# Second feed-forward of a two-layer trunk: the up projection by seven block products, the down projection as one long sum in PSUM

## The chip, the cores and the metric

One core of a Trainium2 chip runs one program. The metric is the device time of one execution in microseconds.

## The reference, cut to what matters

Two layers over 1024 tokens of width 1024, float32. Each layer is a mixer and then a convolutional feed-forward; only the feed-forward of layer 1, the last stage but for a final norm, is touched.

```python
def conv_ffn(h, w_in, conv_w, conv_b, w_out):     # h 1024 x 1024, w_in 1024 x 5632, w_out 2816 x 1024
    up = h @ w_in
    val, gate = jnp.split(up, 2, axis=-1)         # 2816 each
    gate = causal_depthwise_conv(gate, conv_w, width=3) + conv_b
    return (jax.nn.gelu(gate) * val) @ w_out
...
    h = modulated_rmsnorm(x, norm2_g[i], sh2, sc2)
    x = x + g2[:, None, :] * conv_ffn(h, ffn_w_in[i], ffn_conv_w[i], ffn_conv_b[i], ffn_w_out[i])
return rmsnorm(x, final_g).astype(x.dtype)
```

## The kernel before, in words

All activations lie transposed: 128 channels on the partitions, tokens along the free side, in two halves of 512 tokens (`hf`). The residual xT has eight tiles of 128 channels (`KD`). Each float32 factor of a product is split into a rounded high part and a low rest (`split`, L101: ScalarE copies the high part, L105, VectorE subtracts, L106), and one product is three matmuls, high by high, high by low and low by high (`mm3`, L109, its matmuls L115 to L117). So a tile of the up projection over one half is 8 x 3 matmuls of 128 x 512.

The feed-forward (`ffn`, L1382) goes over 11 pairs of tiles (22 tiles of 128, `NF`). For a pair and a half, `up` multiplies two gate and two value tiles, `gate` does the three taps and the GELU, `value` multiplies and splits the result. `down` multiplies the pair's two tiles with the weights of all eight output tiles and adds each sum to xT right away (L1451). Gate and value stay in SBUF. The normed input of half 0 is made during the output projection of half 1 (`out_proj1`, L1375), that of half 1 during the first four up products (`norm_parts`, L566, whose three parts are the sum of squares, the row factors by `rstd_cols` and Newton steps, and the spread over the partitions, L551, with the scaling). At the end `finish` (L1477) transposes each half back, norms it and stores it.

A planner fixes each engine's order before the run, by the order of the code; `high_priority(offset=...)` moves a block's instructions forward by that many. A buffer of a pool is taken again when all that used it is done; the memory of a closed pool is reused in the same way, tile by tile. Loads go through SyncE's queue (SP), stores and re-loads of x through GpSimd's (POOL); each queue issues in its order. In `out_proj` (L1358) the reads of xT (L1370) are put behind the weight loads on SP.

## Time and profile before

| | |
|---|---|
| median of 3 runs | 2573.07 us (2572.48 to 2581.45) |
| profiled execution | 2570.86 us |
| its span, first to last instruction | 2569.2 us |
| mean granted TensorE clock | 0.988 |
| up and down of the second feed-forward on TensorE | from about 1824 us to about 2553 us |

The span is in microseconds from the first instruction. PE is the TensorE matmuls, PEld its weight loads, DVE VectorE, ACT ScalarE, POOL GpSimd, SPq the issue queue of SyncE. A row's line is that of the code; where a helper records the operation, the names of its operands tell the place: `up` and `dn` are the sums of the two projections, `lin` those of the output projection, `h` the normed input, `wH` and `wL` the split weights.

### The profile page before, as it was taken

The page shows a single profiled execution, that of the slowest core. Times are in us where ns is not written, and L with a number is a line of the kernel's source. Part 1 is how long each engine was busy: PE and PEld are TensorE (multiplying, and loading weights), DVE is VectorE, ACT ScalarE, POOL GpSimd, SP SyncE. Part 2 cuts the span into 40 slices and gives each one's busy share as a digit, 9 for nine tenths or more (in the row PEclk, how much of TensorE's full clock was granted, in tenths as well). Part 3 has the DMA queues.
Part 4 walks back from the last instruction along what each step waited for, and adds up shares of the span by engine and source line. Part 5 has one row for each costly group of instructions (what it writes and reads, how often), then busy time and mean ns, then how long its engine had stood idle before and what let it go on. Part 6 is the DMA issues. An engine that isn't in the chain of part 4 may idle for free.

```text
span 2569.2 us, 32004 instructions
## 1 busy us (share of the span) xinstructions
PE 2500.7 (97%) x12127; PEld 2076.3 (81%) x12127; DVE 1580.3 (62%) x3085; ACT 913.9 (36%) x1521; POOL 134.5 (5%) x252
## 2 busy tenths in 40 slices
PE   6999999999999999999999999999999999999998
PEld 5788888887788888888888778787788888888886
DVE  6777776666845595567678554664744444444447
ACT  3655566673322232212224333332421222222222
POOL 1000000040000000000001121210000000000000
PEclk7999999999999999999999999899999999999999
DMA  8455544476412333332233442426211111111111
GB/s 300 132 143 144 149 136 134 140 247 204 143 50 81 102 109 107 110 94 81 81 101 124 152 152 85 154 97 227 75 57 42 49 49 50 45 46 44 47 50 66
DMA packets 260922, 282.43 MB, mean 110 GB/s; under 512 B 21345, under 2 KB 191958, under 8 KB 260256
## 3 DMA queue, kind: packets, MB, share of 16 engines
q1 hardware_dynamic: 240576, 211.64, 27.4%
q0 software_dynamic: 20192, 68.75, 7.7%
q8 instruction: 95, 1.56, 0.3%
q14 instruction: 59, 0.48, 0.1%
HBM read 213.04 MB, written 40.94 MB: 99 GB/s over the span
## 4 chain that ended last, share of the span: by engine, by line
PE 83%; DVE 5%; DMA 4%; issue 3%; ACT 3%; POOL 0%; SPq 0%; DVEq 0%; ACTq 0%; POOLq 0%
PE up L115 12%; PE up L117 12%; PE up L116 12%; PE dn L115 6%; PE dn L117 6%; PE dn L116 6%; PE lin L115 6%; PE lin L116 6%; PE lin L117 6%; PE ta L709 1%; PE S L686 1%; DMA mix<-mixd 1%; PE S L687 1%; DMA pn<-in_mod_w_dram 1%; PE ta L535 1%
## 5 line engine op out<-in xcount | busy, mean ns | idle before, releaser
L115 PE MATMUL up<-h,wH 128*128 128x512 f32 x1408 | 549.7, 390 | 3.0 <-DVE xT L1372 3.0
L116 PE MATMUL up<-h,wH 128*128 128x512 f32 x1408 | 548.1, 389 | 0.0
L117 PE MATMUL up<-h,wL 128*128 128x512 f32 x1408 | 547.9, 390 | 0.2 <-DVE wL L106 0.2
L1451 DVE SCALAR_TENSOR_TENSOR xT<-dn,mod,xT 128x512 f32<-128x512 f32 x352 | 261.4, 748 | 122.0 <-PE dn L117 120.7
L106 DVE TENSOR_TENSOR wL<-stage,wH 128x1024 fp32r<-128x1024 f32 x164 | 199.8, 1221 | 210.3 <-ACT wH L105 206.6
L115 PEld LDWEIGHTS up<-h,wH 128*128 128x128 f32 x1408 | 264.3, 188 | 58.8 <-issue 2.0
L117 PEld LDWEIGHTS up<-h,wL 128*128 128x128 f32 x1408 | 264.3, 188 | 56.1 <-DVE wL L106 1.0
L116 PEld LDWEIGHTS up<-h,wH 128*128 128x128 f32 x1408 | 264.5, 188 | 54.9
L105 ACT ACTIVATE wH<-stage 128x1024 fp32r<-128x1024 f32 x164 | 173.1, 1058 | 310.2 <-PE lin L116 108.2
L115 PE MATMUL dn<-gh,dH 128*128 128x512 f32 x704 | 275.4, 392 | 0.2 <-ACT dH L105 0.2
L117 PE MATMUL dn<-gh,dL 128*128 128x512 f32 x704 | 274.6, 391 | 0.1
L116 PE MATMUL dn<-gl,dH 128*128 128x512 f32 x704 | 274.6, 390 | 0.0
L115 PE MATMUL lin<-h,wH 128*128 128x512 f32 x576 | 235.0, 408 | 7.4 <-ACT h L403 6.6
L116 PE MATMUL lin<-h,wH 128*128 128x512 f32 x576 | 233.9, 406 | 0.0
L117 PE MATMUL lin<-h,wL 128*128 128x512 f32 x576 | 230.6, 401 | 0.0
L1397 ACT ACTIVATE ca<-up,colsB,taps 128x512 f32<-128x512 f32 x84 | 64.9, 772 | 392.1 <-PE up L117 391.9
L115 PEld LDWEIGHTS dn<-gh,dH 128*128 128x128 f32 x704 | 132.1, 188 | 28.6 <-ACT dH L105 0.9
L117 PEld LDWEIGHTS dn<-gh,dL 128*128 128x128 f32 x704 | 132.2, 188 | 27.7 <-DVE dL L106 0.5
L116 PEld LDWEIGHTS dn<-gl,dH 128*128 128x128 f32 x704 | 132.4, 188 | 27.2 <-DVE gl L1415 0.2
L1413 DVE TENSOR_TENSOR ca<-up,ca 128x512 f32<-128x512 f32 x84 | 57.8, 690 | 148.5 <-PE up L117 145.3
L1398 DVE SCALAR_TENSOR_TENSOR ca<-up,taps,ca 128x511 f32<-128x511 f32 x84 | 62.6, 746 | 134.8 <-ACT ca L1397 134.6
L115 PEld LDWEIGHTS lin<-h,wH 128*128 128x128 f32 x576 | 110.6, 192 | 28.8 <-ACT h L403 6.9
(452 smaller groups left out, 3929.8 us busy)
## 6 DMA issues: line engine op xcount, KB each, us to landing
stage<-in_ffn_w_in_dram SPq DMA_DIRECT2D x88, 512.0 KB, 3.8
pn<-in_mod_w_dram SPq DMA_DIRECT2D x160, 256.0 KB, 3.0
stage<-in_ffn_w_out_dram SPq DMA_DIRECT2D x44, 512.0 KB, 3.3
mix<-mixd POOLq DMA_DIRECT2D x60, 256.0 KB, 5.7
stage<-in_ev_w_in_dram SPq DMA_DIRECT2D x24, 512.0 KB, 4.0
mixd<-t2k POOLq DMA_DIRECT2D x44, 256.0 KB, 3.1
mw<-in_mod_w_dram SPq DMA_DIRECT2D x32, 256.0 KB, 5.2
Q<-pn SPq DMA_DIRECT2D x64, 128.0 KB, 2.3
```

The costliest lines, as they stand in the source:

```text
L105: nc.scalar.activation(wh[:, :n], st[:, :n], AF.Copy)
L106: nc.vector.tensor_tensor(wl[:, :n], st[:, :n], f(wh[:, :n]), ALU.subtract)
L115: nc.tensor.matmul(ps, wh, xh, start=s, stop=False)
L116: nc.tensor.matmul(ps, wh, xl, start=False, stop=False)
L117: nc.tensor.matmul(ps, wl, xh, start=False, stop=e)
L535: nc.tensor.matmul(p[:, t:t + 1], accs[t // 4][:, t % 4 * 128:t % 4 * 128 + 128], self.ones, start=True, stop=True)
L686: nc.tensor.matmul(dst, q, KH[:, kk], start=True, stop=False)
L687: nc.tensor.matmul(dst, q, KL[:, kk], start=False, stop=True)
L1397: nc.scalar.activation(a, p, AF.Identity, bias=self.cb[l][:, ft:ft + 1], scale=w2)
L1398: v.scalar_tensor_tensor(a[:, 1:512], p[:, 0:511], w1, a[:, 1:512], ALU.mult, ALU.add)
L1413: nc.vector.tensor_tensor(a, p, a, ALU.mult)
L1451: nc.vector.scalar_tensor_tensor(xT[:, n, hs], p, g2[:, n:n + 1], xT[:, n, hs], ALU.mult, ALU.add)
```

## The change

The up projection of layer 1 is computed by Winograd's form of Strassen's scheme on 2 x 2 blocks. The weights of a tile are four blocks: gate and value (g, v) by the lower and the upper half of the 1024 input channels. The input is four blocks: lower and upper channels by token half (B11, B12 / B21, B22). With T1 = B12 - B11, T2 = B22 - T1, T3 = B22 - B12, T4 = B21 - T2 and S = v_lo + v_hi, the seven products are p1 = g_lo B11, p2 = g_hi B21, p3 = (g_hi - S + g_lo) B22, p4 = v_hi T4, p5 = S T1, p6 = (S - g_lo) T2, p7 = (g_lo - v_lo) T3; the four results are p1 + p2, p1 + p6 + p5 + p3, p1 + p6 + p7 + p4 and p1 + p6 + p7 + p5. Each product is four blocks of 128 by three matmuls.

`up7_blocks` makes the T blocks in place of the normed xT, with a split of each; the first half's norm also writes its result into xT (`keep`), so x is stored to DRAM first (`store_x`) and loaded again for the down projection. The first four tiles (`PRE`) run p1 and p2 ahead. Gate times value goes to DRAM (`Gd`). `down22` runs after all of up: for each half and each group of four output tiles it sums all 22 tiles in four PSUM banks; weights (512 columns) and gate-value (512 columns) are loaded into one stage buffer and split together. There are six stage buffers and three pairs of split buffers. In the output projection before it, the second pair of weight buffers lies in X0 (`Slots`, views of one tile handed out in turn), and xT and the new blocks lie at other addresses than before. `conv` is the taps and GELU as in `gate`, from SBUF. The feed-forward of layer 0 is as it was.

```diff
+PRE = 4
...
         for d in range(KD):
-            t = self.tmp()
+            t = xT[:, d, hs] if keep else self.tmp()
             h, lo = self.hx(d, hf)
             nc.vector.scalar_tensor_tensor(t, xT[:, d, hs], gs[:, d:d + 1], r, ALU.mult, ALU.mult)
-            nc.scalar.activation(h, t, AF.Identity, bias=sh[:, d:d + 1])
-            nc.vector.scalar_tensor_tensor(lo, t, sh[:, d:d + 1], f(h), ALU.add, ALU.subtract)
+            if keep:
+                nc.scalar.activation(t, t, AF.Identity, bias=sh[:, d:d + 1])
+                nc.scalar.activation(h, t, AF.Copy)
+                nc.vector.tensor_tensor(lo, t, f(h), ALU.subtract)
+            else:
+                nc.scalar.activation(h, t, AF.Identity, bias=sh[:, d:d + 1])
+                nc.vector.scalar_tensor_tensor(lo, t, sh[:, d:d + 1], f(h), ALU.add, ALU.subtract)
 
...
-    def out_proj1(self, w, l, xT, x, ps, fetch=False):
-
-        parts = self.norm_parts(xT, 0, l, 1, ps, "lin")
+    def out_proj1(self, w, l, xT, x, ps, fetch=False, keep=False):
+
+        if keep:
+            self.store_x(xT, 0)
+        parts = self.norm_parts(xT, 0, l, 1, ps, "lin", keep)
         next(parts)
         self.out_proj(w, l, xT, 1, x, ps, between=parts, fetch=fetch)
...
+    def up7_blocks(self, l, xT, ps, tag, xb):
+        nc, v = self.nc, self.nc.vector
+        gs, sh = self.gs[l][:, 8:16], self.mod[l][:, 24:32]
+        h0, h1 = slice(0, 512), slice(512, 1024)
+        acc = self.sumsq(xT, h1)
+        yield
+        y = self.rstd_cols([acc], D, ps, tag)
+        yield
+        r = self.spread_cols(y, ps, tag)
+        self.h[1] = X1 = self.new_h(1, "h")
+        X0, X2 = self.xblocks
+        B11, B12, B21, B22 = (xT[:, k:k + 4, h] for k in (0, 4) for h in (h0, h1))
+        T1, T3, T4, T2 = X1[:, :, 0:4], X1[:, :, 4:8], X2[:, :, 0:4], X2[:, :, 4:8]
+        def scale(k):
+            for d in range(k, k + 4):
+                t = xT[:, d, h1]
+                v.scalar_tensor_tensor(t, t, gs[:, d:d + 1], r, ALU.mult, ALU.mult)
+                nc.scalar.activation(t, t, AF.Identity, bias=sh[:, d:d + 1])
+        def low(x, dst):
+            nc.scalar.activation(dst[:, 0], x, AF.Copy)
+            v.tensor_tensor(dst[:, 1], x, f(dst[:, 0]), ALU.subtract)
+        scale(0)
+        v.tensor_tensor(B11, B12, B11, ALU.subtract)
+        scale(4)
+        low(B11, T1)
+        low(B22, X0)
+        v.tensor_tensor(B12, B22, B12, ALU.subtract)
+        v.tensor_tensor(B22, B22, B11, ALU.subtract)
+        low(B22, T2)
+        v.tensor_tensor(B21, B21, B22, ALU.subtract)
+        low(B12, T3)
+        low(B21, T4)
+        yield
+    def up7(self, l, blocks, free, wxs, Gd):
+        nc, v, i = self.nc, self.nc.vector, self.i
+        wi = i["ffn_w_in"][l]
+        def load(pool, n0):
+            st = pool.tile([128, 1024], F32, tag="stage", name="stage", bufs=2)
+            nc.sync.dma_start(st.rearrange("p (t n) -> p t n", n=128),
+                              wi[:, n0:n0 + 128].rearrange("(t p) n -> p t n", p=128))
+            return st
+        with self.pool(f"u7ps{l}", bufs=1, space=PSUM) as ps:
+            bank = lambda k: ps.tile([128, 512], F32, tag=f"c{k}", name=f"c{k}", bufs=(0, 2, 3, 3)[k])
+            prep = blocks(ps, bank)
+            X = {}
+            def operands():
+                h0, X1 = self.h
+                X0, X2 = self.xblocks
+                X.update(B22=at(X0, range(4)), T1=at(X1, range(4)), T3=at(X1, range(4, 8)),
+                         T4=at(X2, range(4)), T2=at(X2, range(4, 8)))
+            at = lambda t, k: [(t[:, 0, n], t[:, 1, n]) for n in k]
+            X.update(B11=at(self.h[0], range(4)), B21=at(self.h[0], range(4, 8)))
+            def product(p, W, o, x, start=True, stop=True):
+                self.mm3(p, [(W[0][:, o + j * 128:o + j * 128 + 128], W[1][:, o + j * 128:o + j * 128 + 128]) + X[x][j]
+                             for j in range(4)], start, stop)
+            def head(ft, q, again=False):
+                with self.tc.high_priority(offset=AHEAD):
+                    early = 2 <= ft < PRE
+                    q["g"] = load(wxs if early and not again else self.wp, (NF + ft) * 128)
+                    if not again:
+                        q["A"] = self.split(q["g"], 1024, *((self.wp, "w", 2) if ft < PRE and ft % 2 else (wxs, "w", 1)))
+            def p1(ft, q):
+                p = bank(1)
+                product(p, q["A"], 0, "B11")
+                q["s1"] = self.tmp(tag="pn")
+                nc.scalar.copy(q["s1"], p)
+            def p2(ft, q):
+                q["c1"] = bank(1)
+                product(q["c1"], q["A"], 512, "B21")
+            def sums(ft, q):
+                with self.tc.high_priority(offset=AHEAD):
+                    g, a = q["g"], load(wxs, ft * 128)
+                    q["s3"] = s3 = self.tmp(tag="ma")
+                    lo, hi = slice(0, 512), slice(512, 1024)
+                    v.tensor_tensor(s3, g[:, lo], a[:, lo], ALU.subtract)
+                    v.tensor_tensor(a[:, lo], a[:, lo], a[:, hi], ALU.add)
+                    q["V"] = self.split(a, 1024, late)
+                    v.tensor_tensor(g[:, lo], a[:, lo], g[:, lo], ALU.subtract)
+                    v.tensor_tensor(g[:, hi], g[:, hi], g[:, lo], ALU.subtract)
+                    q["G"] = self.split(g, 1024, self.wp)
+            def conv(ft, hf, p, q):
...
+            def out(ft, hf, a, val):
+                v.tensor_tensor(a, val, a, ALU.mult)
+                nc.gpsimd.dma_start(Gd[ft][:, hf * 512:hf * 512 + 512], a)
+            def gate0(ft, q):
+                c = self.tmp(tag="ma")
+                v.tensor_tensor(c, q["c1"], q["s1"], ALU.add)
+                q["a0"] = conv(ft, 0, c, q)
+            def p5(ft, q):
+                p = bank(3)
+                product(p, q["V"], 0, "T1")
+                q["s5"] = self.tmp()
+                nc.scalar.copy(q["s5"], p)
+            def p3(ft, q):
+                q["c3"] = bank(3)
+                product(q["c3"], q["G"], 512, "B22")
+            def third(ft, q):
+                with self.tc.high_priority(offset=AHEAD):
+                    q["S3"] = [late.tile([128, 512], F32R, tag=t, name=t, bufs=1) for t in ("s3h", "s3l")]
+                    nc.scalar.activation(q["S3"][0], q["s3"], AF.Copy)
+                    v.tensor_tensor(q["S3"][1], q["s3"], f(q["S3"][0]), ALU.subtract)
+            def p6(ft, q):
+                p = bank(2)
+                product(p, q["G"], 0, "T2")
+                q["u2"] = late.tile([128, 512], F32, tag="u2", name="u2", bufs=1)
+                v.tensor_tensor(q["u2"], p, q["s1"], ALU.add)
+            def p7(ft, q):
+                p = bank(2)
+                product(p, q["S3"], 0, "T3")
+                q["u3"] = late.tile([128, 512], F32, tag="u3", name="u3", bufs=1)
+                v.tensor_tensor(q["u3"], p, q["u2"], ALU.add)
+            def p4(ft, q):
+                p = bank(2)
+                product(p, q["V"], 512, "T4")
+                val = self.tmp()
+                v.tensor_tensor(val, p, q["u3"], ALU.add)
+                out(ft, 0, q["a0"], val)
+            def last(ft, q):
+                v.tensor_tensor(q["u2"], q["s5"], q["u2"], ALU.add)
+                v.tensor_tensor(q["s5"], q["s5"], q["u3"], ALU.add)
+                v.tensor_tensor(q["u2"], q["c3"], q["u2"], ALU.add)
+                out(ft, 1, conv(ft, 1, q["u2"], q), q["s5"])
+            Q = [{} for _ in range(NF + 2)]
+            next(prep)
+            for ft in range(PRE):
+                head(ft, Q[ft])
+                p1(ft, Q[ft])
+                if ft == 0:
+                    next(prep)
+                p2(ft, Q[ft])
+                if ft == 0:
+                    next(prep)
+                if ft > 1:
+                    c = self.tmp()
+                    nc.scalar.copy(c, Q[ft]["c1"])
+                    Q[ft]["c1"] = c
+            operands()
+            free()
+            with self.pool(f"late{l}", bufs=1) as late:
+                for ft in range(2):
+                    sums(ft, Q[ft])
+                    p5(ft, Q[ft])
+                    p3(ft, Q[ft])
+                    gate0(ft, Q[ft])
+                third(0, Q[0])
+                for ft in range(NF):
+                    q, n, m = Q[ft], Q[ft + 1], Q[ft + 2]
+                    p6(ft, q)
+                    if ft + 2 < NF:
+                        head(ft + 2, m, ft + 2 < PRE)
+                        if ft + 2 >= PRE:
+                            p1(ft + 2, m)
+                    p7(ft, q)
+                    if ft + 1 < NF:
+                        third(ft + 1, n)
+                    if ft + 2 < NF:
+                        sums(ft + 2, m)
+                        if ft + 2 >= PRE:
+                            p2(ft + 2, m)
+                        gate0(ft + 2, m)
+                    p4(ft, q)
+                    last(ft, q)
+                    if ft + 2 < NF:
+                        p5(ft + 2, m)
+                        p3(ft + 2, m)
+    def down22(self, l, xT, Gd, wb, wc, ps, mid):
+        nc = self.nc
+        wo = self.i["ffn_w_out"][l]
+        g2 = self.mod[l][:, 40:48]
+        parts = None
+        steps = itertools.count()
+        for hf in range(2):
+            hs = slice(hf * 512, hf * 512 + 512)
+            for nh in range(2):
+                pss = [ps.tile([128, 512], F32, tag="acc", name="acc", bufs=6) for _ in range(4)]
+                for k in range(NF):
+                    s = next(steps)
+                    with self.tc.high_priority(offset=2 * AHEAD):
+                        st = (self.wp if s < 4 or s % 3 == 0 else wc).tile([128, 1024], F32, tag="stage", name="stage",
+                                                                           bufs=2 if s < 4 or s % 3 == 0 else 4)
+                        nc.sync.dma_start(st[:, 0:512], wo[k * 128:k * 128 + 128, nh * 512:nh * 512 + 512])
+                        nc.sync.dma_start(st[:, 512:1024], Gd[k][:, hs])
+                        W = self.split(st, 1024, (self.wp, self.wp, wb, wb, wc, wc)[s % 6])
+                    x = W[0][:, 512:1024], W[1][:, 512:1024]
+                    for n in range(4):
+                        ns = slice(n * 128, n * 128 + 128)
+                        self.mm3(pss[n], [(W[0][:, ns], W[1][:, ns]) + x], start=k == 0, stop=k == NF - 1)
+                    if parts and k in (2, 6):
+                        next(parts, None)
+                for n in range(4):
+                    d = nh * 4 + n
+                    nc.vector.scalar_tensor_tensor(xT[:, d, hs], pss[n], g2[:, d:d + 1], xT[:, d, hs], ALU.mult, ALU.add)
+            if hf == 0:
...
+    def last_layer(self, nc):
+        with contextlib.ExitStack() as es:
+            blocks, wxs = (es.enter_context(self.pool(n, bufs=1)) for n in ("xb", "wxs"))
+            X0 = blocks.tile([128, 2, 4, 512], F32R, name="X0")
+            X2 = blocks.tile([128, 2, 8, 512], F32R, name="X2")
+            self.xblocks = X0, X2
+            xe = contextlib.ExitStack()
+            xT = xe.enter_context(self.pool("xp2", bufs=1)).tile([128, KD, L], F32, name="xT")
+            with self.pool("opps1", bufs=4, space=PSUM) as ps:
+                w4 = X0.rearrange("p a b n -> p (a b n)").rearrange("p (a n) -> p a n", n=1024)
+                self.wpools = [self.wp, Slots(wH=[w4[:, 0], w4[:, 1]], wL=[w4[:, 2], w4[:, 3]])]
+                x = lambda t, hf: self.hx(t ^ 4, hf)
+                w = self.i["od_w_out"][0]
+                self.out_proj(w, 1, xT, 0, x, ps, 2, (4, 5, 6, 7, 0, 1, 2, 3), fetch=True, ahead=160)
+                self.out_proj1(w, 1, xT, x, ps, fetch=True, keep=True)
+                self.wpools = [self.wp]
+                self.store_x(xT, 1)
+            Gd = self.dr.tile([NF, 128, L], F32, name="Gd1")
+            class Banks:
+                def __init__(self, bank):
+                    self.tile = lambda *a, **k: bank(2)
+            self.up7(1, lambda ps, bank: self.up7_blocks(1, xT, Banks(bank), "x", None), xe.close, wxs, Gd)
+        with self.pool("xp3", bufs=1) as xp, self.pool("fin", bufs=1) as fin, self.pool("wb", bufs=2) as wb, \
+                self.pool("wc", bufs=2) as wc:
+            xT = self.load_x(xp)
+            self.fgb = fin.tile([128, 4 * D], F32, name="fgb")[:, 0:D]
+            fg = self.i["final_g"]
+            nc.gpsimd.dma_start(self.fgb, bass.AP(tensor=fg.tensor, offset=fg.offset, ap=[[0, 128], [1, D]]))
+            with self.pool("dnps", bufs=2, space=PSUM) as ps:
+                self.down22(1, xT, Gd, wb, wc, ps, lambda ps, tag: self.finish(xT, 0, ps, tag))
+            with self.pool("finps", bufs=4, space=PSUM) as ps:
+                list(self.finish(xT, 1, ps, "fin"))
 
```

## Rows read from the trace of the kernel before

**Rows 1.** Page, part 1: busy us (share of the span) and instructions, by engine
```profile
PE 2500.7 (97%) x12127; PEld 2076.3 (81%) x12127; DVE 1580.3 (62%) x3085; ACT 913.9 (36%) x1521; POOL 134.5 (5%) x252
```
**Rows 2.** Page, part 4: shares of the chain that ended last, by engine
```profile
PE 83%; DVE 5%; DMA 4%; issue 3%; ACT 3%; POOL 0%; SPq 0%; DVEq 0%; ACTq 0%; POOLq 0%
```
**Rows 3.** Windows: us, busy (instructions) of PE PEld DVE ACT POOL, clock, DMA share, GB/s
```profile
1880.00:2000.00 120.00, 120.00 (x531) 99.34 (x530) 54.53 (x74) 26.04 (x37) 0.00 (x0) 1.00 0.15 44
2000.00:2100.00 100.00, 100.00 (x443) 82.78 (x442) 44.34 (x62) 20.05 (x30) 0.00 (x0) 1.00 0.14 43
```
**Rows 4.** Timeline of TensorE: start us, duration us, what
```profile
1845.27 0.39 PE L116 MATMUL up<-h,wH 128*128 128x512 f32 x1
1845.50 0.39 PE L117 MATMUL up<-h,wL 128*128 128x512 f32 x1
```
**Rows 5.** Page, part 5: group, count | busy us, mean ns | idle before, releaser
```profile
L115 PE MATMUL up<-h,wH 128*128 128x512 f32 x1408 | 549.7, 390 | 3.0 <-DVE xT L1372 3.0
L1451 DVE SCALAR_TENSOR_TENSOR xT<-dn,mod,xT 128x512 f32<-128x512 f32 x352 | 261.4, 748 | 122.0 <-PE dn L117 120.7
```
**Rows 6.** Groups by shape, VectorE, 1860 to 2495 us
```profile
L106 DVE TENSOR_TENSOR wL<-stage,wH 128x1024 fp32r<-128x1024 f32 x40 | 49.0, 1225 | 72.9 <-ACT wH L105 71.2
L1399 DVE SCALAR_TENSOR_TENSOR ca<-up,taps,ca 128x510 f32<-128x510 f32 x38 | 28.4, 749 | 1.3
L1413 DVE TENSOR_TENSOR ca<-up,ca 128x512 f32<-128x512 f32 x38 | 26.3, 691 | 86.0 <-PE up L117 84.4 <-ACT ca L1407 1.6
L1405 DVE SCALAR_TENSOR_TENSOR ca<-halo,taps,ca 128x2 f32<-128x2 f32 x19 | 4.0, 210 | 0.0
```
**Rows 7.** Timeline of VectorE: like instructions in a row, and one wait
```profile
1769.47 2.35 DVE L106 TENSOR_TENSOR wL<-stage,wH 128x1024 fp32r<-128x1024 f32 x2
1841.81 2.06 DVE L581 SCALAR_TENSOR_TENSOR t2k<-xT,gs,x 128x512 f32<-128x512 f32 x3 [4.98 <-PE x L551]
1857.88 1.28 DVE L1415 TENSOR_TENSOR gl<-ca,gh 128x512 fp32r<-128x512 f32 x2
1894.99 0.69 DVE L1415 TENSOR_TENSOR gl<-ca,gh 128x512 fp32r<-128x512 f32 x1 [0.70 <-ACT gh L1414]
```
**Rows 8.** Groups by shape, ScalarE, 1860 to 2495 us
```profile
L105 ACT ACTIVATE wH<-stage 128x1024 fp32r<-128x1024 f32 x39 | 41.3, 1060 | 86.2 <-DMA stage<-in_ffn_w_in_dram 43.9 <-PE up L116 38.3 <-PE dn L116 3.9
L1397 ACT ACTIVATE ca<-up,colsB,taps 128x512 f32<-128x512 f32 x38 | 29.3, 771 | 189.3 <-PE up L117 189.3
```
**Rows 9.** Timeline of TensorE at the start of the up projection
```profile
1826.69 0.50 PE L115 MATMUL up<-h,wH 128*128 128x512 f32 x1 [1.42 <-DVE xT L1372]
...
1841.18 0.60 PE L551 MATMUL x<-ident,rs 128*128 128x128 f32 x4
```
**Rows 10.** Timeline of VectorE: end of the sum of squares, last Newton step
```profile
1828.82 0.68 DVE L563 TENSOR_TENSOR ma<-ma,t2k 128x512 f32<-128x512 f32 x1
...
1836.67 0.16 DVE L205 SCALAR_TENSOR_TENSOR rs<-rs 128x4 f32<-128x4 f32 x1
```
**Rows 11.** Windows at the program's start
```profile
40.00:44.00 4.00, 0.75 (x7) 0.67 (x6) 3.28 (x6) 2.17 (x4) 0.00 (x0) 0.61 1.05 398
44.00:48.00 4.00, 2.96 (x6) 2.07 (x7) 3.52 (x6) 2.01 (x4) 0.00 (x0) 0.50 1.06 407
...
52.00:56.00 4.00, 4.00 (x30) 3.65 (x29) 3.82 (x7) 0.00 (x0) 0.00 (x0) 1.00 0.75 227
```
**Rows 12.** Page, part 6: issues, KB each, median us to landing
```profile
stage<-in_ffn_w_in_dram SPq DMA_DIRECT2D x88, 512.0 KB, 3.8
pn<-in_mod_w_dram SPq DMA_DIRECT2D x160, 256.0 KB, 3.0
...
xs<-xT POOLq DMA_DIRECT2D x16, 256.0 KB, 3.7
```
**Rows 13.** Windows: a stretch full of transfers
```profile
532.00:536.00 4.00, 4.00 (x27) 3.43 (x26) 3.23 (x10) 3.50 (x10) 3.03 (x6) 1.00 1.05 407
```
**Rows 14.** Timeline of SyncE's queue before the output projection
```profile
1734.50 9.19 SPq L1370 DMA_DIRECT2D xT<-xs  x2
```

More of the change, by code (lines that the diff above doesn't have):

```diff
@@ L1 @@
+import contextlib
 import itertools
@@ L74, in f, with __init__, tile @@
     return ap.bitcast(F32)
+class Slots:
+    def __init__(self, **tags):
+        self.tags = {k: itertools.cycle(v) for k, v in tags.items()}
+    def tile(self, shape, dt, tag, name, bufs):
+        return next(self.tags[tag])
 class Trunk:
@@ L564, in sumsq, with norm_parts @@
         return acc
-    def norm_parts(self, xT, hf, l, which, ps, tag):
+    def norm_parts(self, xT, hf, l, which, ps, tag, keep=False):
         nc = self.nc
@@ new lines, in down22 @@
+    def down22(self, l, xT, Gd, wb, wc, ps, mid):
[25 more added lines that the diff above has]
+                    nc.vector.scalar_tensor_tensor(xT[:, d, hs], pss[n], g2[:, d:d + 1], xT[:, d, hs], ALU.mult, ALU.add)
+            if hf == 0:
+                parts = mid(ps, "x")
+                next(parts)
+        self.wpools = [self.wp]
@@ L1534, in run @@
                 self.mixer1()
[L1535 to L1551 removed]
+            self.last_layer(nc)
```

31 lines of the change are left out of this document (14 added, 17 removed).

## Prediction

> **What bounds the kernel now.** I read the totals first: TensorE is busy for 97% of the span, VectorE 62%, ScalarE 36% [rows 1]. The chain of work that ended last is 83% TensorE [rows 2]. A busy TensorE need not be a dense one, so next come the stretches of the second feed-forward: a 120 us stretch and a 100 us stretch have no idle time on TensorE at full granted clock, VectorE busy 45% and 44% of them, ScalarE some 21%, the DMA engines 15% [rows 3]. The time order of the matmuls then gives the true price: the mean of one is 390 ns by its group [rows 5], but starts follow each other by 0.227 us [rows 4], since they overlap. So this stage is bound by the count of matmuls times 0.227 us, and a removed matmul is worth 0.227 us, not 0.39.
>
> At this point a rule of the Trainium skill would give another sum. Its page TensorE: Matmul & The Clock Gate (Back-to-back issue gap) gives some 131 ns per matmul of 512 columns as the sustained spacing of load and matmul pairs; by it the 264 matmuls below would be worth an estimated 35 us, not 60. The trace does not agree: 227 ns [rows 4].
>
> **What is removed.** Before, each of the 22 tiles of the up projection takes gate and value x 2 token halves x 8 blocks of 128 x 3 terms = 96 matmuls. After, 7 products x 4 blocks x 3 = 84. The products of the first four tiles that run ahead (p1, p2) are not run again; only their weights are loaded a second time. So 22 x 12 = 264 matmuls go: 264 x 0.2267 = 59.9 us. The down projection has 22 x 8 x 2 x 3 = 1056 matmuls before and 22 x 4 x 4 x 3 = 1056 after: nothing. On VectorE, 176 evictions per layer of 0.75 us (352 for both layers [rows 5]) become 16, but they lay under matmuls: nothing on the path.
>
> The profiled execution took 2570.86 us (span 2569.2, 1.7 around it); the median of three is 2573.07, 2.2 more. From the profiled one: 2570.9 - 59.9 = 2511.0, if nothing new appears.
>
> **What is added in the loop.** Per tile TensorE now has 84 x 0.2267 = 19.0 us. VectorE gets fourteen 512-wide adds or subtractions (four in `sums`, one each in `third`, `gate0`, p6, p7, p4, three in `last`, two in `out`), four taps, three 1024-wide splits and two small ones. In a row these take 0.64, 0.69 and 1.18 us each [rows 7], the small ones about 0.2: 14 x 0.64 + 4 x 0.69 + 3 x 1.18 + 0.4 = 15.7 us; alone, at 0.69, 0.75 and 1.22 [rows 6], 16.8. That is 82% to 88% of TensorE's 19.0 us, against 45% now. ScalarE: three splits at 1.06 and two affines at 0.77 [rows 8], two GELUs and three copies taken as an affine: 8.6 us, free. DMA: 1.5 MB per 19 us = 80 GB/s, far under the 407 GB/s of a full stretch [rows 13].
> So VectorE doesn't bound the loop by its sum. It can by its order: it works strictly behind its own queue, and each wait for ScalarE's half of a split costs it idle time (0.70 us in a case of now [rows 7]) that had no price before. PSUM allows some slack: c2 has three banks for p6, p7, p4, so TensorE can be about two products (5.4 us) ahead. The tightest place is p5 of tile ft+2: its weights use two slots, and the older is freed only when p4 of tile ft ends; then come a ScalarE copy and a VectorE subtraction (1.06 + 1.22 us), while p3 (2.7 us) can cover. Bounds: 0, and 2.3 us x 20 tiles = 46 us. I take 0.25 us per tile, 5 us, near zero because p3 and p6 don't need that slot.
>
> **What is added at the entry.** Before, TensorE starts the up projection at about 1824.4 us and only 1.4 us are lost there, behind the last eviction [rows 9]; the other half's norm is done under 96 matmuls (21.8 us). After, the cover is eight products of 12 matmuls, also 21.8 us, but VectorE has far more to do. The sum of squares ends at 1829.5 [rows 10]; in the old order the row factors then went through the newton steps to 1836.8 [rows 10] and the spread came on TensorE at 1841.2 [rows 9], placed late. The new order asks for it after the second product, so I put the factors at 1835. From there VectorE has: eight scalings (0.69, 5.5); four block differences and five splits of 2048 columns, a width that the trace doesn't have: two 1024-wide in a row take 2.35 us [rows 7], four 512-wide ones 2.6; I take 2.35, so 21.2; two weight splits 2.4; `sums` of tiles 0 and 1 (4 x 0.64 + 2 x 1.18 = 4.9 each) 9.8; two `gate0` 4.0; `third` 0.6; then tiles 0 and 1 of the loop, without a first split, 14.5 each: 29.0. Together 72.5 us, to 1907.5. TensorE's work to the same point is 22 products x 2.72 = 59.8 us plus 1.5 of small ones, to 1885.7. It cannot be ahead of VectorE by more than its banks, some 5 us: it loses 1907.5 - 1885.7 - 5 = 17 us. It loses them mostly in one place: the weights of p5 lie in memory of xT (pool `late`, which opens after xT is given up), and xT is read until the last two of the five splits; until then only p3 and p6 of two tiles (10.9 us) are there to run.
> After an idle spell the clock is lower: where TensorE was busy for 0.75 of 4 us the granted clock was 0.61 and in the next 4 us 0.50, its 1.2 GHz level, and full only from 52 us on [rows 11]. Half clock over some 4 us costs 2 us; I take 1 on top, so 18. Bounds: 6 (VectorE's work on tile 1 can wait, the factors come at 1831) and 30 (factors at 1841 as now, two idle spells).
>
> **The rest.** The first half's norm gets one ScalarE copy more per block (8 x 0.63) and is needed only at 1824: nothing, TensorE has out-projection products till then; uncovered, 5 us. The stores of x go out on POOL's queue, behind which only one broadcast load stood; in-place scaling must wait for them, and each lands in 3.7 us [rows 12], several before it is needed: nothing; late by one landing, 4 us. xT now lies over other memory of the mixer, so its first reads can start later; already now SP stands 9.19 us at such a read [rows 14], with the weight loads behind it: 0 to 6, I take 1.
> Turn from up to down: first loads and splits have old slots, stage buffer 5 and the third pair of weight buffers lie over `late`, freed about 6 to 13 us after p4 of the last tile; four steps of 2.72 us cover 10.9. 0 to 8, I take 3.
> Down: per step of 12 matmuls (2.72 us) ScalarE has 1.06, VectorE 1.22, and 512 KB land: 193 GB/s. Full stretches carried 407 [rows 13]; one 256 KB load takes 3.0 us and a 512 KB one 3.8 [rows 12], and six stages allow six steps (16 us). The 4 MB of x come back beside it, needed only after the first group (60 us). 0 to 12, I take 2. Four banks are evicted at the end of a group, one per 0.68 us as they finish, as the last product of a tile does now; the closing norm stays as it is: nothing, within 2.
>
> Sum: 2511 + 5 + 18 + 1 + 3 + 2 = 2540.
>
> **Rivals.**
> *Entry covered*, 2522: the planner moves the second norm forward and finds products enough. For it: VectorE has idle time before 1824. Against: the last eviction sets the sum of squares, and 26.7 us of block work behind it can't move. 2540 - 18. Chance 0.12.
> *Down fed late*, 2562: each step waits for its two loads. For it: 193 GB/s is four times what this stage moves now. Against: half of what full stretches carry. 0.25 us x 88 = 22 us over the forecast. Chance 0.14.
> *VectorE's order bounds the loop*, slower than before: 16.8 us of lone durations, plus 0.7 us behind each of the eight ScalarE products of a tile that VectorE reads (three splits, the half of `third`, two affines, two GELUs), is 22.4 us. (22.4 - 19.0) x 20 = 68 instead of 5: 2603. It decides from 21.6 us per tile: 52 us there and 24 of other costs (18 + 1 + 3 + 2) make 2587, which is 0.5% over the median of before. Against: other work is there to fill such waits. Chance 0.10; half of it, 2570, no change: 0.06.
> *No fewer matmuls*: by the count of the code 84 per tile, so under 0.01.
>
> **How the numbers follow.** The forecast has 0.57 by itself, with its own range 2526 to 2556. Faster by over 0.5% (which is about what a measurement can tell) means under 2560: the forecast, the covered entry and half of the late loads: 0.76. Within 0.5% (2560 to 2586): the other half, the half VectorE bound and 0.01 unnamed: 0.14. Slower: 0.10. The range that leaves out 2 in 10 reaches from a covered entry with only the loop's 5 us (2511 + 5) to the half-bound loop and some of the late loads: 2516 to 2578.
>
> **What would show it.** Right: 264 fewer TensorE matmuls; a loop whose tiles follow each other by 19 to 19.5 us with VectorE over 80% busy; idle TensorE of 10 to 25 us between 1840 and 1885, released by VectorE's block splits or the first V split; a lower granted clock only there; the down part dense, about 240 us. Wrong: tiles of over 20 us with VectorE's waits on ScalarE in them, TensorE waiting for stage loads in the down part, or no gap at the entry.

## The result, and the profile after

The changed kernel takes 2543.5 us (median of 4 runs, 2542.5 to 2546.4) beside 2577.3 of the kernel before in the same comparison: ratio 0.987, 95% interval 0.985 to 0.990. The profiled execution took 2542.69 us, with a span of 2540.7. The medians differ by 33.8 us, but the runs of the kernel before spread by 9 us here (2572.5 to 2581.8); by the lengths of the stages, below, the change is worth some 27 us. The forecast was 2540, the range 2516 to 2578: faster, and near the size. Its terms were less good than their sum.

First the totals of the page, part 1, of the changed kernel.

```profile
PE 2453.4 (97%) x11863; PEld 2032.5 (80%) x11863; DVE 1709.3 (67%) x3234; ACT 1033.5 (41%) x1646; POOL 175.3 (7%) x328
```

Against [rows 1] TensorE has 12127 - 11863 = 264 matmuls less, just the number counted. VectorE has 129 us more to do. Now windows of the up projection's loop (columns as in [rows 3]), and what VectorE waited for from 1900 to 2255 us (total us, times, longest).

```profile
2000.00:2100.00 100.00, 100.00 (x442) 82.23 (x441) 80.09 (x125) 40.47 (x58) 5.81 (x12) 1.00 0.27 87
```
```profile
DVE u L1644 <- PE c L129: 56.5, 17, 3.3
DVE u L1638 <- PE c L129: 7.4, 18, 1.9
DVE wL L118 <- ACT wH L117: 3.4, 19, 0.3
```

VectorE rose from 44% to 80%, but TensorE is as dense as in [rows 3], and VectorE waits for TensorE, not the reverse: 56.5 us for p7's matmuls, 3.4 us in all for ScalarE's half of the splits. So the loop costs nothing.

To find the rest I cut each trace at four places of TensorE's timeline: the last wait of the mixer, the first and the last matmul of the up projection, the last of the down projection. I call the stages between them seam, up and down, and what follows the tail; the entry is the start of up, the turn is where up gives way to down. The first fence is the kernel before, the second the changed one (start us, duration us).

```profile
1735.24 0.50 PE L115 MATMUL lin<-mix,wH 128*128 128x512 f32 x1 [0.85 <-DVE pn L1352]
...
1824.43 0.39 PE L115 MATMUL up<-h,wH 128*128 128x512 f32 x1
...
2552.55 0.39 PE L117 MATMUL dn<-gh,dL 128*128 128x512 f32 x1
```
```profile
1733.48 0.50 PE L127 MATMUL lin<-mix,wH 128*128 128x512 f32 x1 [0.86 <-DVE pn L1369]
...
1829.80 0.39 PE L127 MATMUL c<-h,wH 128*128 128x512 f32 x1
...
2265.81 0.39 PE L129 MATMUL c<-X,wL 128*128 128x512 f32 x1
...
2522.40 0.39 PE L129 MATMUL acc<-wH,wL 128*128 128x512 f32 x1
```

| stage, us | before | changed | control (e11) | seam and turn mended (e10) |
|---|---|---|---|---|
| seam: mixer's last wait to first up matmul | 89.2 | 96.3 | 96.7 | 92.4 |
| up: to the end of its last matmul | 728.5 with down | 436.4 | 436.2 | 436.4 |
| down: to the end of its last matmul | in the row above | 256.6 | 257.7 | 244.8 |
| tail: to the end of the span | 16.3 | 17.9 | 17.9 | 17.5 |
| sum | 834.0 | 807.2 | 808.5 | 791.1 |

Of what was lost against the 59.9 us, the seam holds 7.1, the tail 1.6, and up and down together 59.9 - (728.5 - 693.0) = 24.4. What TensorE waited for from 1690 to 2541 us names the places:

```profile
PE acc L127 <- ACT wH L117: 7.9, 1, 7.9
PE lin L127 <- ACT wH L117: 5.7, 1, 5.7
PE c L127 <- ACT t2k L1671: 3.2, 1, 3.2
PE c L128 <- DVE X L1521: 3.1, 1, 3.1
PE c L127 <- ACT X L1520: 1.9, 1, 1.9
PE acc L127 <- DVE t2k L1650: 1.4, 1, 1.4
```

The waits of `acc` are at the turn, the wait of `lin` at the seam, and those of `c` at the entry. At the turn: ScalarE's row (the split that ended that wait), VectorE's last operation on the up projection's output, GpSimd's queue (x coming back, and the last store of that output), and the windows:

```profile
2285.48 4.85 ACT L117 ACTIVATE wH<-stage 128x1024 fp32r<-128x1024 f32 x5 [9.74 <-DMA xT<-xs]
```
```profile
2274.83 0.69 DVE L1610 TENSOR_TENSOR ca<-t2k,ca 128x512 f32<-128x512 f32 x1 [0.76 <-ACT ca L1606]
```
```profile
2270.89 2.12 POOL L1836 DMA_DIRECT2D xT<-xs  x4
2274.22 0.54 POOL L1836 DMA_DIRECT2D xT<-xs  x1 [1.21 <-DMA Gd<-ca]
2278.03 0.55 POOL L1611 DMA_DIRECT2D Gd<-ca  x1 [3.28 <-DMA xT<-xs]
```
```profile
2276.00:2280.00 4.00, 2.73 (x13) 1.92 (x11) 1.00 (x1) 0.00 (x0) 1.32 (x3) 1.00 1.03 412
2280.00:2284.00 4.00, 0.00 (x0) 0.00 (x0) 0.00 (x0) 0.00 (x0) 2.18 (x5) 0.59 1.04 415
2284.00:2288.00 4.00, 0.95 (x2) 0.44 (x2) 1.43 (x2) 2.52 (x3) 1.06 (x3) 0.50 0.94 379
```

The engines stand while the DMA engines run full at 412 and 415 GB/s. What ended ScalarE's wait is a transfer on GpSimd's queue. By the built program's semaphores that split (the fifth step's) waits for two of the stores there, since its weight buffer lies over `ca`, from which the output is stored. The last store was ready at 2275.5, stood behind x's loads on the queue until 2278.0, and landed 7.4 us later, at 2285.4; the split started 0.1 us after that. The granted clock is then 0.50, its 1.2 GHz level.

### The profile page after: what moved, and what is told of

Read it like the earlier page. It is cut to its first block, busy times and chain, and to the rows that moved or that the text cites. A ratio compares the mean times of both kernels' runs of the same rounds, so it can differ in the third digit from the quotient of the medians.

```text
span 2540.7 us, 32400 instructions
## 1 busy us (share of the span) xinstructions
PE 2453.4 (97%) x11863; PEld 2032.5 (80%) x11863; DVE 1709.3 (67%) x3234; ACT 1033.5 (41%) x1646; POOL 175.3 (7%) x328
## 4 chain that ended last, share of the span: by engine, by line
PE 83%; DVE 5%; DMA 4%; ACT 3%; issue 3%; SPq 1%; POOL 0%; DVEq 0%; ACTq 0%; POOLq 0%
PE lin L127 7%; PE lin L128 7%; PE lin L129 7%; PE up L127 6%; PE up L129 6%; PE up L128 6%; PE c L129 5%; PE c L128 5%; PE c L127 5%; PE dn L127 3%; PE dn L129 3%; PE dn L128 3%; PE acc L128 3%; PE acc L129 3%; PE acc L127 3%
## 5 line engine op out<-in xcount | busy, mean ns | idle before, releaser
L127 PE MATMUL up<-h,wH 128*128 128x512 f32 x736 | 287.6, 391 | 1.6 <-DVE xT L1389 1.2
L128 PE MATMUL up<-h,wH 128*128 128x512 f32 x736 | 286.7, 390 | 0.0
L129 PE MATMUL up<-h,wL 128*128 128x512 f32 x736 | 286.0, 390 | 0.0
L127 PEld LDWEIGHTS up<-h,wH 128*128 128x128 f32 x736 | 138.2, 188 | 31.1 <-issue 1.6
L1470 DVE SCALAR_TENSOR_TENSOR xT<-dn,mod,xT 128x512 f32<-128x512 f32 x176 | 130.5, 746 | 45.7 <-PE dn L129 45.3
L128 PEld LDWEIGHTS up<-h,wH 128*128 128x128 f32 x736 | 138.3, 188 | 28.6
L127 PE MATMUL acc<-wH 128*128 128x512 f32 x352 | 138.5, 393 | 9.2 <-ACT wH L117 7.9
L127 PE MATMUL dn<-gh,dH 128*128 128x512 f32 x352 | 138.5, 394 | 0.4 <-DVE xT L1470 0.4
L128 PE MATMUL acc<-wL,wH 128*128 128x512 f32 x352 | 137.9, 392 | 0.5 <-DVE wL L118 0.5
L129 PE MATMUL dn<-gh,dL 128*128 128x512 f32 x352 | 138.0, 392 | 0.0
L128 PE MATMUL dn<-gl,dH 128*128 128x512 f32 x352 | 137.7, 391 | 0.0
L129 PE MATMUL acc<-wH,wL 128*128 128x512 f32 x352 | 137.6, 391 | 0.0
```

The costliest lines, as they stand in the source:

```text
L127: nc.tensor.matmul(ps, wh, xh, start=s, stop=False)
L128: nc.tensor.matmul(ps, wh, xl, start=False, stop=False)
L129: nc.tensor.matmul(ps, wl, xh, start=False, stop=e)
L1470: nc.vector.scalar_tensor_tensor(xT[:, n, hs], p, g2[:, n:n + 1], xT[:, n, hs], ALU.mult, ALU.add)
```

## The experiments

Times are medians; "before" is the kernel before beside the runs. The program ahead of the mixer's last wait, whose products no kernel here alters, took 1733.5 to 1741.5 us in the fourteen profiles, while a stage that is left alone repeats to 0.8 us (seam 96.0 to 96.7, up 436.2 to 437.0), down to 1.9 (255.8 to 257.7, mean 256.5 of nine, the changed kernel's own 256.6). The expectations count down from its first matmul, 0.2 us earlier than here: their 256.8 and 253.5 are 256.6 and 253.3 below. So a few us are judged by the stage lengths; the medians stand beside them.

**e11, the control: the changed kernel itself.**

> The changed kernel once more, unaltered, beside the others. By every theory 2537 to 2546 us, and the same lengths of its stages as in its first profile (96.3, 436.4 and 256.8 us) to within 1 us; what the start of the program takes may differ by some us.

2545.5 us beside 2576.1 (ratio 0.990, 0.987 to 0.992). Seam 96.7, up 436.2, down 257.7, 1.1 above the first profile, so 0.1 beyond what was named.

**e4: is the loop bound by TensorE?** The fifth product twice.

```
                 p = bank(3)
                 product(p, q["V"], 0, "T1")
+                product(p, q["V"], 0, "T1")
```

> The fifth product of each of the 22 tiles is done twice (the first result is overwritten): 264 matmuls more, so as many as in the kernel before, with the new kernel's work on the other engines. Theory (TensorE sets the loop's pace; 0.2267 us for a matmul): +59.9 us less the 0 to 3 us that the first two tiles hide at the entry, 2600 to 2604. Rival (VectorE's order sets the pace in half of the tiles): +30 us, 2573. If the loop is bound by VectorE altogether: 0 to +10 us.

2602.9 us beside 2571.5 (ratio 1.011, 1.009 to 1.014); up 495.6 us, 59.2 more: 0.224 us for each of the 264. The gain is the removed matmuls, at the full price. Without the saving the new arrangement is 31 us slower than the old one: about the 33 us lost at entry, seam, turn and tail.

**e7: how much room has VectorE?**

```
                 q["a0"] = a = conv(ft, 0, c, q)
+                for _ in range(4):
+                    v.tensor_tensor(a, a, a, ALU.max)
```

> Four operations of 512 columns more on VectorE in each of the 22 tiles (maximum of the gate's convolution with itself), 0.61 us each in a row, 2.4 us a tile, so 17.6 of 19.0 us instead of 15.2. Theory (TensorE sets the loop's pace and VectorE has slack): 436.4 to 439 us from the first to the last product of the up projection. Rival (VectorE's order is at its limit in part of the tiles): +20 to +50 us.

2545.6 us beside 2571.3 (ratio 0.990, 0.989 to 0.992); up 438.4, 2.0 more for 54 us of added work. Its loop:

```profile
2000.00:2100.00 100.00, 100.00 (x441) 82.15 (x441) 92.32 (x144) 40.23 (x58) 5.94 (x11) 1.00 0.27 85
```

At 92% VectorE still doesn't hold TensorE.

**e6: is the entry VectorE's work?** Two of its 2048-wide subtractions left out (low parts of T1 and T2 used for T3 and T4).

```
-        low(B12, T3)
-        low(B21, T4)
+        nc.scalar.activation(T3[:, 0], B12, AF.Copy)
+        nc.scalar.activation(T4[:, 0], B21, AF.Copy)
...
+                         T3=[(X1[:, 0, n], X1[:, 1, n - 4]) for n in range(4, 8)],
+                         T4=[(X2[:, 0, n], X2[:, 1, n + 4]) for n in range(4)])
```

> Leaves out the low parts of two of the five operands made at the entry (T3's and T4's; the low parts of T1 and T2 are used in their place), so two operations of VectorE of 2.2 us each; matmuls and all else stay. From the first to the last product of the up projection the new kernel takes 436.4 us. Theory (VectorE's chain at the entry sets when the first V weights may land on x's memory): 4.4 us less, 432. Rival (ScalarE's copies and their order, or the banks): 0 to 1 us less.

2544.1 us beside 2571.3 (0.989, 0.986 to 0.991); up 433.1, so 3.3 us less, three quarters of the 4.4 taken from VectorE. Its chain is the main bound of the entry; not all of it reaches TensorE.

**e8: two tiles of cover in place of four** (`PRE = 2`).

> Two tiles instead of four have their first two products computed ahead of the blocks, so TensorE has 24 x 2 matmuls, 10.9 us, less to do while VectorE makes the blocks. Theory (VectorE's chain is as long as before less two splits of 1.1 us; TensorE waits for its end): 8 to 11 us more from the first to the last product of the up projection, 444 to 447. Rival (the two early tiles, with their copies on ScalarE and second loads, cost what they cover): 435 to 438.

2553.1 us beside 2571.3 (ratio 0.994, 0.992 to 0.995); up 441.3, 4.9 more: between the two theories. The four tiles do cover, but of the 10.9 us moved only half shows. Part of the rest is what the two tiles bring with them: the wait of 3.2 us for their copies on ScalarE (L1671) doesn't occur here, and VectorE has two splits less; what each is worth was not separated. The changed kernel's entry in windows, then this kernel's, then one window of the control's:

```profile
1840.00:1850.00 10.00, 8.54 (x37) 6.41 (x35) 9.79 (x11) 8.43 (x12) 0.00 (x0) 1.00 0.18 54
1850.00:1860.00 10.00, 6.03 (x24) 4.35 (x24) 10.00 (x6) 5.78 (x6) 0.00 (x0) 1.00 0.00 0
1860.00:1870.00 10.00, 5.81 (x18) 4.36 (x18) 7.91 (x6) 5.79 (x7) 0.00 (x0) 0.83 0.18 52
```
```profile
1850.00:1860.00 10.00, 8.01 (x22) 5.80 (x22) 9.96 (x6) 6.39 (x6) 0.00 (x0) 0.66 0.01 2
1860.00:1870.00 10.00, 5.90 (x14) 3.66 (x12) 8.02 (x5) 3.82 (x2) 0.00 (x0) 0.66 0.00 0
```
```profile
1850.80:1860.80 10.00, 6.99 (x18) 5.08 (x19) 10.00 (x6) 5.77 (x6) 0.00 (x0) 0.66 0.00 0
```

In both VectorE is full (10.00 and 9.96 of 10 us). In e8 TensorE's busy time from 1850 to 1870 is as much or more, but with 36 matmuls in place of 42 (43 in the changed kernel's like stretch, which lies 5.2 us earlier): it runs at a granted clock of 0.66. A window at that clock need not cost anything, though. The control is the same kernel as the changed one. In the like window it ran at 0.66 and not at 1.00, with 18 matmuls in place of 24; it had less idle time at the entry (8.0 us, not 10.2), and its up took 436.2 us beside 436.4. So in this pair the low clock only took time that TensorE otherwise spent waiting.

**e3: one low part on GpSimd.**

```
-        def low(x, dst):
+        def low(x, dst, e=v):
...
-            v.tensor_tensor(dst[:, 1], x, f(dst[:, 0]), ALU.subtract)
+            e.tensor_tensor(dst[:, 1], x, f(dst[:, 0]), ALU.subtract)
...
-        low(B12, T3)
+        low(B12, T3, nc.gpsimd)
```

> One of the five low parts at the entry of the up projection (T3's, 2048 wide, 2.29 us on VectorE) is computed on GpSimd. Theory (VectorE's 31 us without a gap from 1835.8 to 1866.8 set when TensorE gets T2, and when the memory of x comes free for the first V weights): the first split of V ends 2.2 us earlier and the time falls by about 2 us, 2541 to 2542. Rival (the wait is the two copies of the early tiles' products on ScalarE and their banks): no change, 2543 to 2544. If GpSimd slows VectorE while it runs, the gain is lost or turns to a loss of 1 to 3 us.

2548.6 us beside 2571.5 (ratio 0.991, 0.989 to 0.993); up 439.1, a loss of 2.7. GpSimd's row and VectorE's at the same time:

```profile
1856.05 4.60 POOL L1521 TENSOR_TENSOR h<-xT,h 128x2048 fp32r<-128x2048 f32 x1 [22.85 <-ACT h L1520]
```
```profile
1856.13 5.61 DVE L118 TENSOR_TENSOR wL<-stage,wH 128x1024 fp32r<-128x1024 f32 x1
1861.67 2.28 DVE L1528 TENSOR_TENSOR xT<-xT 128x2048 f32<-128x2048 f32 x1
```

VectorE's split, 1.22 us elsewhere, took 5.61: it started 0.08 us after GpSimd's operation and ended 1.1 us after it, as if it only began when GpSimd was done.

**e2: the two early up loads at the seam.**

```
-                    q["g"] = load(wxs if early and not again else self.wp, (NF + ft) * 128)
+                    with self.tc.issue_after(self.loaded) if early and not again else contextlib.nullcontext():
+                        q["g"] = load(wxs if early and not again else self.wp, (NF + ft) * 128)
```

> The two early loads of up weights (tiles 2 and 3), which now stand between the first loads of the output projection on the queue, are issued behind its last load. Theory (these two loads of 512 KB compete with the weights of the output projection's first tiles, 15.12 us from wait to arrival): the first product of the output projection waits about 5 us less and the time falls by 4 to 6 us to 2537.5 to 2539.5. Rival (the seam is late because the queue stands 11.83 us in its second read into xT, whose memory comes free only when the mixer is done): 0 to -2 us, 2541.5 to 2545.

2543.5 us beside 2571.5 (ratio 0.988, 0.986 to 0.990); seam 95.8, 0.2 below the lowest of the unaltered ones. My theory fell; the loads are worth well under 1 us.

**e5: in addition, x is read behind the next pair of weights.**

```
+        get = lambda n0: [self.weights(w, 0, n * 128, ahead=AHEAD if n0 else ahead) for n in range(n0, n0 + group)]
+        nxt = get(0) if group == 2 else None
...
-            Ws = [self.weights(w, 0, n * 128, ahead=AHEAD if n0 else ahead) for n in ns]
+            Ws = nxt or get(n0)
+            nxt = get(n0 + group) if group == 2 and n0 + group < KD else None
             if fetch:
                 with self.tc.issue_after(self.loaded):
...
```

> As e2_heads, and in the output projection's first half the loads of x are issued behind the weights of the next pair of tiles, not of their own. From the end of the mixer's wait (the idle of 0.86 us before the last pass over its last tile) to the first product of the up projection the new kernel takes 96.3 us, e2_heads 95.8, the kernel before 89.2. Theory (the weights of the second pair share the DMA engines with 1 MB of x and 0.5 MB of up weights that did not stand beside them before, and the queue stands 11.83 us in a read into x's memory ahead of the next weights): 90 to 93 us, the time 2 to 5 us below e2_heads by the trace. Rival (the burst is the mixer's own 5 MB, and what x brings changes little): 95 to 96 us.

2541.0 us beside 2571.3 (ratio 0.989, 0.987 to 0.990); seam 92.4, 3.4 less than e2 and 3.9 less than the changed kernel. SyncE's queue before the change, of the changed kernel, and of e5 (a duration includes what the queue stood there, and the first row of e5 holds one load of the first pair and, from 1732.0, the second pair):

```profile
1718.67 0.81 SPq L1370 DMA_DIRECT2D xT<-xs  x2
```
```profile
1728.86 0.89 SPq L1387 DMA_DIRECT2D xT<-xs  x2
1729.80 0.43 SPq L1542 DMA_DIRECT2D stage<-in_ffn_w_in_dram  x1
1731.12 4.87 SPq L103 DMA_DIRECT2D stage<-in_od_w_out_dram  x2
1736.03 11.83 SPq L1387 DMA_DIRECT2D xT<-xs  x2
```
```profile
1716.69 16.81 SPq L103 DMA_DIRECT2D stage<-in_od_w_out_dram  x3
1733.81 9.84 SPq L1390 DMA_DIRECT2D xT<-xs  x2
```

Before, the first two reads of x went out at 1718.7. In the changed kernel they and a load of up weights go out from 1728.9, just ahead of the second pair of weights at 1731.1, into a stretch that fills up; in e5 the weights go first. ScalarE's wait for the first of these weights, again before the change, of the changed kernel and of e5, and TensorE's wait in e5:

```profile
1745.47 1.06 ACT L105 ACTIVATE wH<-stage 128x1024 fp32r<-128x1024 f32 x1 [9.62 <-DMA stage<-in_od_w_out_dram]
```
```profile
1749.20 1.06 ACT L117 ACTIVATE wH<-stage 128x1024 fp32r<-128x1024 f32 x1 [15.12 <-DMA stage<-in_od_w_out_dram]
```
```profile
1746.19 1.06 ACT L117 ACTIVATE wH<-stage 128x1024 fp32r<-128x1024 f32 x1 [11.21 <-DMA stage<-in_od_w_out_dram]
```
```profile
1747.30 0.50 PE L127 MATMUL lin<-mix,wH 128*128 128x512 f32 x1 [1.72 <-ACT wH L117]
```

So the weights' wait falls from 15.12 to 11.21 us, and TensorE's at the seam from 5.66 to 1.72.

**e1: the load of x out of the turn.**

```
-            xT = self.load_x(xp)
+            xT = xp.tile([128, KD, L], F32, name="xT")
...
+                    if k in (8, 10, 12, 14):
+                        d = nh * 4 + (k - 8) // 2
+                        with self.tc.issue_after(ld):
+                            nc.sync.dma_start(xT[:, d, hs], self.xs[:, d, hs])
```

> The eight tiles of x for each half are loaded one at a time behind the stage loads of the ninth, eleventh, thirteenth and fifteenth step of the group of the down projection that needs them, not all at its start; nothing else is changed. Theory (the 4 MB of x come back beside the first loads of the down projection; the split at 2285.48 waited 9.74 us for a load and the first products had 1.35 and 7.86 us of idle before them): the idle time at the turn falls from about 10.5 to 1 to 3 us, the time to 2533 to 2537 against 2543.5. Rival (the stage and weight buffers, which lie where the up projection's V weights lay, come free late): the waits at the turn stay, and the time stays within 2541 to 2546.

2541.4 us beside 2571.5 (ratio 0.988, 0.986 to 0.990); down 253.3, 3.3 under the changed kernel's 256.6. TensorE's idle time at the turn shrank by half, from 9.7 to 5.0 us, and the rest stayed: neither theory alone. In e1: VectorE, TensorE, GpSimd's queue, ScalarE:

```profile
2271.24 1.23 DVE L118 TENSOR_TENSOR wL<-stage,wH 128x1024 fp32r<-128x1024 f32 x1 [2.47 <-ACT wH L117]
...
2272.99 0.68 DVE L1650 TENSOR_TENSOR t2k<-c,u 128x512 f32<-128x512 f32 x1
```
```profile
2273.72 0.80 PE L127 MATMUL acc<-wH 128*128 128x512 f32 x1 [3.45 <-DVE t2k L1650]
```
```profile
2280.62 0.54 POOL L1611 DMA_DIRECT2D Gd<-ca  x1 [4.92 <-DVE ca L1610]
```
```profile
2284.78 4.85 ACT L117 ACTIVATE wH<-stage 128x1024 fp32r<-128x1024 f32 x5 [4.22 <-issue]
```

VectorE stood 2.47 us before a split of the down weights, whose load was not in; L1650, queued behind it, empties the PSUM bank that the down sums need, so TensorE stood 3.45 us. The last store now goes out 0.3 us after VectorE's last operation on that output ends (at 2280.33), it lands 4.0 us later, and the fifth step's split starts 0.1 us after that.

**e9: the order of the first down loads as well.**

```
+                self.lastv = v.tensor_tensor(q["u2"], q["c3"], q["u2"], ALU.add).ins
...
+                        own = s < 6 or s > 9 and s % 3 == 0
+                        st = (self.wp if own else wc).tile([128, 1024], F32, tag="stage", name="stage", bufs=2 if own else 4)
+                        with self.tc.issue_after(ld) if 0 < s < 22 else contextlib.nullcontext():
...
+                        with self.tc.issue_after(self.lastv) if s == 3 else contextlib.nullcontext():
+                            W = self.split(st, 1024, (self.wp, self.wp, wb, wb, wc, wc)[s if s < 4 else (s - 4) % 6])
```

> As e1_turn, and the down projection's first loads go out in the order of their steps: in e1_turn the tenth step's load stood on the queue ahead of the fifth's and waited for a buffer that the fourth's split frees, and five loads left together at 2272.5 to 2278 and came in together at 2284.8; the split of the fourth step stood on VectorE ahead of the last tile's evictions, whose banks the first sums need (3.45 us of idle). Now the fifth and sixth steps use the stage buffers of the common pool, weights rotate from the oldest on, and that split stands behind the last tile's evictions. Theory (two in-order engines are blocked behind a wait for a DMA): TensorE's idle at the turn falls from 5 to 1 to 3 us, and the time from the first to the last product of the down projection from 253.5 to 250 to 252 us (256.8 in the new kernel). Rival (the DMA engines are full with 3 MB at the turn, whatever the order): 253 to 254.

2533.7 us beside 2576.1 (ratio 0.984, 0.982 to 0.987); down 245.2, 8.1 under e1 and more than I expected. One sentence of the expectation was a wrong reading: five splits in a row don't show that their loads came in together. By the built program's semaphores the first of them waited for the stores out of `ca`; here the fifth to eighth steps take the oldest weight buffers, and the buffers over `ca` come up only at the ninth. The turn in one window, changed kernel, then e9, each from 4.2 us ahead of the end of up:

```profile
2262.00:2300.00 38.00, 28.32 (x115) 22.31 (x114) 21.81 (x28) 12.01 (x13) 11.23 (x21) 0.87 0.93 327
```
```profile
2267.83:2305.83 38.00, 37.37 (x165) 30.60 (x164) 26.67 (x32) 16.76 (x18) 2.65 (x5) 1.00 0.87 301
```

50 matmuls more in the same 38 us, at full clock. The queue's order, the rotation of the buffers and the place of the one split were changed together; which does most was not separated.

**e12: the order alone, x back at the start** (e9 without the edit of e1).

> e9_turn2 with the load of x put back where the changed kernel has it, all 16 tiles at the start of the down projection: the order of the queue and of VectorE is mended, the 4 MB of x still come beside the first loads. From the last product of the up projection to the last of the down projection the changed kernel takes 256.6 and 257.7 us in two profiles, e1_turn (only x moved) 253.3, e9_turn2 (both) 245.2. Theory (the two causes add up: x is worth 3.3 us, the order 8.1): 248 to 250 us. Rival (with the order mended the stage loads are early enough and x is harmless): 245 to 246. Second rival (x alone fills the DMA engines at the turn, so the order helps only once x is out of the way): 253 to 257.

2537.2 us beside 2575.3 (ratio 0.986, 0.983 to 0.989); down 250.4. From the changed kernel's 256.6: x alone 3.3, order and buffers alone 6.2, both 11.4 us. About a sum; the 1.9 us that only both together give are no more than the spread of this stage. 250.4 lies just above the first theory's band, and both rivals are out.

**e10: e5 and e9 together.**

> e5_seam and e9_turn2 together. Theory (the seam and the turn add up): 3.9 us less from the mixer's last wait to the up projection, 5 to 7 us less in the down projection, so 9 to 11 us under the new kernel beside it, 2530 to 2535 where that is at 2541 to 2544. Rival (the gains are given back at the next stage): 2537 to 2543.

2533.0 us, beside 2545.5 of the changed kernel and 2576.1 of the kernel before: ratio to before 0.983 (0.981 to 0.986), which does not overlap the control's 0.987 to 0.992. By stages 16 to 17 us less, seam 92.4 and down 244.8, nothing given back; between the medians it is 12.5. The start of its profiled execution took 4.6 us more than the control's (1738.5 against 1733.9), and whether that is chance is not shown. This version beats both kernels.

## Why the prediction came out as it did

- **264 matmuls at 0.2267 us, -59.9**: right, by the count of the page and by e4 (59.2 us back). In e4 one costs 0.224 us. The Trainium skill, TensorE: Matmul & The Clock Gate (Back-to-back issue gap), has some 131 ns, with which no run here agrees.
- **The loop, +5**: nothing. The order was feared with 16.8 of 19.0 us; measured 80% with VectorE waiting for TensorE, and e7 shows room up to 92%. The rival "VectorE's order bounds the loop" is out.
- **The entry, +18**: up and down without the turn leave 24.4 - 11.4 = 13, by subtraction, so with all else that differs there. The mechanism is the one forecast, in the main: VectorE is without a gap, and TensorE has 10.2 us of idle time in six waits between 1846 and 1871, of which 5.6 us are for T2 and the first V split. The 2048-wide operations took 2.28, as the 2.35 taken. One step of the sum did not hold: it let VectorE's work on tiles 0 and 1 (29.0 of the 72.5 us) hold TensorE too, but after 1871 TensorE has no wait of over 0.1 us up to the end of up. Not foreseen were the other 4.6 us, for copies of the early tiles' products on ScalarE: the longest (L1671, 3.23 us, for a bank) stands behind a 2048-wide operation. The 1 us for the clock is not borne out: the granted clock was 0.83 in one window here and 0.66 in the control's, and up came out the same.
- **The seam, +1**: 7.1, above the bounds of 0 to 6. The step that said "already now SP stands 9.19 us" [rows 14] saw the place and not the price: the first pair of x reads, which before went out at 1718.7, now goes out at 1728.9, into the mixer's own burst and next to the second pair of weights. e5 shows 3.9 of the 7.1; the other 3.2 are open.
- **The turn, +3, and x's return in the +2 for down**: 11.4 together by e9, against 5; these are the worst-sized terms. The turn's own part, order and buffers, is 6.2 us with x left where it was (e12) and 8.1 with x moved (e9 against e1), at the upper end of its bounds of 0 to 8. The place was right (weight buffers over `late`), the time was not: "freed about 6 to 13 us after p4 of the last tile" was 19 us after its end (2266.2 to 2285.5). VectorE's last operation ended 9.3 us after p4, within those 6 to 13; the last store, of which the step says nothing, then stood 2.5 us on GpSimd's queue and took 7.4 to land. Nor did the forecast ask what stands behind a waiting split on VectorE: in e1 that is a PSUM eviction, for which TensorE stood 3.45 us.
- **Down, +2**: the part that was weighed, feeding, costs nothing: 244.8 us in e10 against 1056 x 0.2267 = 239.4 of bare pitch, so "down fed late" is out. But "the 4 MB of x come back beside it, needed only after the first group" priced x by when it is needed. It takes the DMA engines when it is issued: 3.3 us alone (e1), 5.2 on top of a mended order (e12 against e9). Those 5.2 lie at the turn: in e9's window of 38 us there, e12 has 142 matmuls and e9 165.
- **The tail, within 2**: 1.6. VectorE before, then after:

```profile
2551.61 0.75 DVE L1451 SCALAR_TENSOR_TENSOR xT<-dn,mod,xT 128x512 f32<-128x512 f32 x1
2552.28 0.68 DVE L563 TENSOR_TENSOR ma<-ma,t2k 128x512 f32<-128x512 f32 x1
2552.98 0.75 DVE L1451 SCALAR_TENSOR_TENSOR xT<-dn,mod,xT 128x512 f32<-128x512 f32 x1
```
```profile
2520.79 2.80 DVE L1730 SCALAR_TENSOR_TENSOR xT<-acc,mod,xT 128x512 f32<-128x512 f32 x4 [11.96 <-PE acc L129]
2523.50 0.68 DVE L575 TENSOR_TENSOR ma<-ma,t2k 128x512 f32<-128x512 f32 x1
```

Evictions used to alternate with the sums of squares; now four come together and the sums follow.

Of the signs named, two went against the forecast: the clock fell at the turn too (0.50), not only at the entry, and the down part began with 9.7 us of idle time.

So 10 us too much (loop 5, entry 5) stood against 14 too little (seam 6, turn and down 6, tail 2). The forecast had -30.9 in all; by stages it is -26.8, and the profiled execution shows -28.2 (2570.86 to 2542.69) because its start was 1.8 us shorter. The size owes as much to errors that offset as to insight.

## What to carry to other kernels

Price a removed matmul by the pitch of starts in a dense stretch, and look for what is lost at the joints between stages, where the pitch does not hold. At a joint, follow a reused buffer back to the last transfer that reads it, with what stands ahead of that transfer on its queue and what fills the DMA engines while it flies; and list for each in-order queue what stands ahead of the first thing that the next stage needs. When a reload is needed says nothing about when it takes bandwidth: put it behind the urgent loads.

## What the runs showed of the hardware

- A GpSimd operation on 2048 columns (two inputs) took 4.60 us, twice VectorE's 2.28, and VectorE's two-input operation that started 0.08 us later ended 1.1 us after it (5.61 in place of 1.22 us). The Trainium skill, SBUF — State Buffer (SBUF: two separate sides), calls the pair's shared port an exclusive lock: whoever starts first holds it for the whole instruction. This trace agrees, in the one case that it has.
